# Value products of two quads in one group, eight buffers of transposed probabilities, and later last products in a hybrid attention block

## The chip, the cores and the metric

The kernel runs on one core of a Trainium2 chip. The metric is the device time of one execution in microseconds. Five engines work side by side, each on its own queue of instructions in order: TensorE (PE in the profile; its weight loads are the row PEld), VectorE (DVE), ScalarE (ACT), GpSimd (POOL) and SyncE (SP), which issues nearly all DMA transfers. Semaphores order them among each other.

## The reference, cut to what matters

One encoder layer on 1024 tokens of width 1024: one input projection, two groups of eight attention heads of 64 columns each, a gate, an output projection, a residual and a layer norm.

```python
h = jnp.einsum('bsd,de->bse', x, w_in[layer])
q_a, k_a, v_a, z_a, q_b, k_b, v_b, z_b = jnp.split(h, SPLIT_POINTS, axis=-1)
y_a = neighborhood_attention(q_a, k_a, v_a, rel_pos_bias[layer])      # window 8 x 16 on a 16 x 64 grid
y_b = windowed_gqa_with_sink(rotary(q_b), rotary(k_b), v_b, sink_logits[layer])   # |i - j| <= 128
mixed = jnp.concatenate([y_a * jax.nn.silu(z_a), y_b * jax.nn.silu(z_b)], axis=-1)
y = jnp.einsum('bse,ed->bsd', mixed, w_out[layer])
x = layer_norm(DEEPNORM_ALPHA * x + y, ln_gain[layer], ln_bias[layer])
```

In each attention the probabilities are a softmax over a row's keys, and the output is probabilities times values. Reshapes are left out above.

## The kernel before, in words

Nearly all matmuls are in 16 bits: each operand is split into a high and a low half, and three products (high-high, high-low, low-high) stand for one product in 32 bits. So one block of the input projection is 8 x 3 matmuls of 128x512 (`project`, L381, its matmul L404), and the output projection has the same form (`out_mms`, L1155, its matmul L1165).

**Prologue.** The values of all heads are projected first, the inputs and the weights are scanned for scales (`x_turn`, L514, turns a column of maxima into a row with a matmul against the identity), and six of the 21 blocks of the input projection are made.

**The attention loop** (L1328) runs over 128 units in steps i. A unit is one head and 128 queries: the first 64 units are the windowed group ("b"), the last 64 the neighbourhood group ("a"). Four units that follow each other make a quad. For each unit:

- `stage_mm` (L924, matmul L933) makes the scores of a whole quad in four banks of PSUM, tag "s", of which there are five. A head has 64 columns, so these matmuls use 64 rows of the array, and two heads go side by side on its two halves. `batch(i + 1)` issues them at each step with i % 4 == 3, for the quad that begins at the next step.
- `stage_qk` (VectorE, L958) adds bias or mask and finds the row's extreme, `stage_exp` (ScalarE, L974) takes the exponential, `stage_sum` (VectorE, L980 and L981) the reciprocal of its sum.
- `stage_tr` (L985) splits the probabilities into halves (ScalarE L992, VectorE L993), which frees the bank, and issues a DMA on SP that transposes them into a tile `tr` (L999). A quad has two such tiles; there are BH = 6, those of three quads.
- `stage_pv` (L1005, matmul L1035) multiplies the transposed probabilities of a quad by the values: 18 or 24 matmuls that use 64 columns of the array, two heads side by side. Results lie in one half of the bank "t", by the parity of the quad. `PV_AT` (L1321) says at which step a quad's products are issued: quad q at step 4q + 11, right behind the scores of a later quad; quads 30 and 31 at 131 and 135, where no scores are left.
- `stage_z` (L1037, VectorE L1043 and L1046) multiplies that by the gate, in place, at the steps of `Z_AT`.

**Fill.** Between these groups TensorE works on `fill`, a list of generators: the other 15 blocks of the input projection (48 matmuls each) and then parts of the output projection (`out_head`, L1171). `pump_to(u)` (L1056) issues as many of these matmuls as the table FILL_AT gives for the step u; WARP bends the four steps of a quad. What the loop leaves over goes out at its end (L1414).

**The other engines' queues** are lists as well; `pop` takes a few operations per step, and `need` takes one that is about to be used. Weight blocks are loaded on SP (`w_load`, L200), split on ScalarE (L214) and GpSimd (L219, L220). The output weights come in 16 loads (`wo_load`, L1100) at the steps WO_LD into raw tiles with the tags WO_TAG, and are scanned and split (`wo_split`, L1111). Six of them are loaded earlier too, for their scan only, into four buffers of tag "wos" (`wo_pre_load`, L804); the last two of these scans are at steps 12 and 20. `gather_v` (L846) loads the values of the next head pair for one column block, one step behind the products that were the last to use that block of the pair before.

**The end** (`final`, L1182). Here the order is no longer written out by hand. The gated outputs of the "a" heads are split into m tiles (ScalarE L1076, VectorE L1077), first the tokens below 512, then the rest; the other weights are split (L1121 to L1134, and L1191 on GpSimd); one more bank, tag "t", gets its first half of the sum (12 matmuls); then eight open banks get the second half, one head pair e after the other, three matmuls for each bank and e; then the remaining blocks, the residual (L1215) and the norm.

Of the kernel before, what the change touches and what calls it, by code (L numbers as in the profile page):

```python
# [25 lines left out]
QSCALE = 2.0 ** -15  # L26
BH, BR, NX, F1 = 6, 6, 6, 0.2
NSPLIT, NP = 6, 2
# [12 lines left out]
FILL = ORDER[NPRO:]  # L41
FILL_AT = [0, 6.6, 13.4, 21.4, 29.4, 37.4, 45.4, 53.4, 61.4, 70, 78.8, 87.6, 96.4, 105, 113, 122, 125, 127, 128.5, 131.5, 136]
ZTAG = {"z3": "zv", "zb3": "zc", "z2": "zs", "zb1": "zd", "zb2": "ze"}
# [4 lines left out]
VA_AT = [46, 49, 52, 55]  # L48
WO_TAG = ("wor", "wor", "raw", "raw") + ("wr",) * 5 + ("wor", "wor", "raw", "raw", "raw", "wr", "wr")
M_AT = [64, 72, 80, 88]  # L50
WO_PRE = (9, 10, 12, 13, 14, 15)
WO_POST = (7, 8)
WO_MAX = 88
EO = (4, 5, 6, 7, 0, 1, 2, 3)
LAST = ((0, 384), (384, 128))
# [19 lines left out]
def hybrid_block(ctx, tc, xT, x, wt, wv, wo, bias, sink, gain, lbias, cos, sin, bmask, out):  # L75
# [5 lines left out]
    wp = ctx.enter_context(tc.tile_pool(name="wp", bufs=3))  # L81
# [56 lines left out]
    wos = const.tile([128, 1], F32, name="wos")  # L138
# [297 lines left out]
    with ExitStack() as vctx:  # L436
# [77 lines left out]
        def x_turn(ps):  # L514
            nc.tensor.matmul(ps[:, 320:448], gm.to_broadcast([128, 128]), identf, start=False, stop=True,
                             skip_group_check=True)

# [99 lines left out]
        for k in range(KT):  # L617
# [6 lines left out]
            for ps in FIRST if k == 0 else SECOND if k == 1 else ([(t, a, i) for i in range(3)] for t, a in T1):  # L624
# [5 lines left out]
                if k > 1:  # L630
                    g = T1.index((t, a))
# [200 lines left out]
    rawp = ctx.enter_context(tc.tile_pool(name="rawp", bufs=3, reuse_waits="tile"))  # L832
# [168 lines left out]
    def quad(q):  # L1001
        g, p, j, t = units[4 * q]
        return g, p, t // 2 if g == "b" else t[0]
# [48 lines left out]
    fill.extend(project(n) for n in FILL)  # L1052
    FILL_N = [48] * len(FILL) + [9, 9, 6, 12, 24]
    pumped = [0]

    def pump_to(u):  # L1056
        n = 0
        k = int(u) % 4
        u = int(u) // 4 * 4 + 4 * (WARP[k] + (WARP[k + 1] - WARP[k]) * (u - int(u)))
        for k, c in enumerate(FILL_N):  # L1060
            u0, u1 = FILL_AT[k], FILL_AT[k + 1]
            n += int(c * min(max((u - u0) / (u1 - u0), 0), 1))
        pump(n - pumped[0])
        pumped[0] = max(n, pumped[0])
# [35 lines left out]
    def wo_load(n):  # L1100
        if n < 16:
            tag = WO_TAG[n]
            pool, bufs = (rawp, 3) if tag == "raw" else (wp, {"wr": 5, "wor": 2}[tag])
            raw = pool.tile([128, 512], F32, tag=tag, name=f"wor{n}", bufs=bufs)
            e, a = WO_SEQ[n]
            nc.sync.dma_start(raw, wo[e, :, 512 * a:512 * a + 512])
            wo_raw[n] = raw
# [44 lines left out]

    LO = 10
    NU = len(units)
# [165 lines left out]

    PV_AT = {4 * q + 11: q for q in range(30)}  # L1321
    PV_AT.update({131: 30, 135: 31})
    Z_AT = {4 * q + 13: q for q in range(30) if q not in (24, 25, 28, 29)}
    Z_AT.update({115: 24, 116: 25, 128: 28, 129: 29, 132: 30, 136: 31})

    clock["step"] = 0
    scan_ops = []
    for i in range(-LD, NU + LO):  # L1328
# [15 lines left out]
        if i in PRE_AT:  # L1344
            n = len(WO_PRE) - len(PRE_AT) + PRE_AT.index(i)
# [44 lines left out]
        pump_to(i + F1)  # L1390
        if i - 1 in PV_AT and quad(PV_AT[i - 1])[0] == "a":
            _, p, b = quad(PV_AT[i - 1])
            if p < 3:
                gather_v(p + 1, b)
        free = 2 if i % 4 > 1 or i >= NU else 0
        turned = pop("dve", free if i < 105 else 1 + free)
        if i % 4 == 0 and i < NU:
            stage_exp(units[i])
        if i in PV_AT or i % 4 == 3 and i + 1 < NU:
            if i < NU:  # L1400
                stage_sum(units[i - 1:i + 1])
            pump_to(i + QK_AT)
            if i + 1 < NU:
                batch(i + 1)
            if i in PV_AT:
                stage_pv(PV_AT[i])
            if i + 1 < NU:
                stage_qk(units[i + 1])
# [83 lines left out]
```

## Time and profile before

| | us |
|---|---|
| median of 3 runs | 439.92 |
| lowest and highest of them | 439.67, 441.48 |
| the profiled execution's own time | 441.73 |
| its span, first to last instruction | 439.90 |
| mean granted TensorE clock | 0.998 of full speed |
| first scores of the loop | 122.8 |
| first and last value products | 145.5, 361.7 |

The profile is of one execution. A row of a timeline has the start and the length in us, the engine, the line of the kernel, the operation, the tile written and those read, the shape and the count; what the engine idled for stands in brackets. Rows that follow each other with the same line and shape are merged, and the length is then that of all of them. A length ends at the modelled end of the last instruction; matmuls are pipelined, so the next one starts before that.

### The profile page before, as it was taken

To read this page: it belongs to the slowest core of one execution; us is meant where nothing else is said; L and a number is where in the kernel's file an instruction comes from. 1 tells how busy PE (TensorE), PEld (TensorE's weight loads), DVE (VectorE), ACT (ScalarE), POOL (GpSimd) and SP (SyncE) were. 2 spreads that over 40 slices of the span, in tenths; PEclk is the share of its full clock that TensorE was granted. 3 is DMA by queue.
4 is the path that set the end of the run, shared out by engine and by line. 5 is a ranking of instruction groups with operands and counts; after the bars stand their busy time and mean duration, and the time that the engine had idled before them with its cause. 6 is when DMAs were issued, how large, how long until landed. Compare 5 with 4: busy or idle time off the path is not lost. (4 is left out here: it accounts for less than half of the span.)

```text
span 439.9 us, 8798 instructions
## 1 busy us (share of the span) xinstructions
PE 431.2 (98%) x2955; PEld 233.2 (53%) x2955; DVE 347.8 (79%) x897; ACT 298.8 (68%) x697; POOL 212.7 (48%) x204
## 2 busy tenths in 40 slices
PE   9999999999999999999999999999999989999994
PEld 8987754444444545454545455554545544444442
DVE  5999947929989988988888887887879739089954
ACT  6798359877577988877889899879787756002211
POOL 0305743564845868356333455566652158005840
PEclk9999999999999999999999999999999999999999
DMA  8992088967946978776999899999999979101721
GB/s 296 343 339 71 5 259 250 302 247 254 322 113 136 168 147 171 141 145 143 173 154 201 138 190 223 192 202 217 216 208 225 193 166 363 41 1 72 262 74 72
DMA packets 133981, 81.72 MB, mean 186 GB/s; under 512 B 101296, under 2 KB 113328, under 8 KB 133680
## 3 DMA queue, kind: packets, MB, share of 16 engines
q1 hardware_dynamic: 133504, 80.67, 74.4%
q8 instruction: 23, 0.38, 0.3%
q10 hardware_dynamic: 432, 0.49, 0.3%
q14 instruction: 22, 0.18, 0.1%
HBM read 50.73 MB, written 9.96 MB: 138 GB/s over the span
## 5 line engine op out<-in xcount | busy, mean ns | idle before, releaser
L404 PE MATMUL ps_pj<-xf,wh 128*128 128x512 f16 x672 | 201.2, 379 | 0.0
L404 PE MATMUL ps_pj<-xf,wl 128*128 128x512 f16 x336 | 127.5, 380 | 0.0
L404 PEld LDWEIGHTS <-wh 128*128 128x128 f16 x672 | 64.9, 98 | 75.4 <-issue 0.8
L1165 PEld LDWEIGHTS <-m 128*128 128x128 f16 x408 | 38.7, 98 | 43.7
L974 ACT ACTIVATE ps_s<-sn,nm 128x385 f32<-128x385 f32 (+3 forms) x96 | 52.1, 543 | 13.9 <-DVE nm L958 12.5
L992 ACT ACTIVATE split<-ps_s,ri 128x384 f16<-128x384 f32 (+2 forms) x96 | 48.5, 539 | 18.3 <-ACT ps_s L974 11.7
L993 DVE SCALAR_TENSOR_TENSOR split<-ps_s,ri,split 128x384 f16<-128x384 f32 (+2 forms) x96 | 52.0, 570 | 5.6 <-ACT split L992 4.6
L1165 PE MATMUL ps_s<-wo,m 128*128 128x512 f16 (+1 forms) x240 | 53.3, 374 | 0.0
L404 PEld LDWEIGHTS <-wl 128*128 128x128 f16 x336 | 32.8, 98 | 38.5 <-issue 0.3
L219 POOL TENSOR_SCALAR wr<-wr,wsc 128x512 f32<-128x512 f32 x26 | 22.4, 862 | 46.9 <-ACT wh L214 45.5
L958 DVE CUSTOM_DVE_ANT_0 sn<-ps_s,bm,nsk 128x384 f32<-128x384 f32 (+1 forms) x64 | 39.7, 635 | 6.6 <-PE ps_s L933 6.4
L901 POOL TENSOR_SCALAR bias<-bias,rsg 128x552 f32<-128x552 f32 (+1 forms) x24 | 20.0, 834 | 45.8 <-DMA bias<-in_bias 33.9
L958 DVE CUSTOM_DVE_ANT_0 sn<-ps_s,bias,sg 128x264 f32<-128x264 f32 (+1 forms) x64 | 33.9, 543 | 2.3 <-PE ps_s L933 1.6
L933 PE MATMUL ps_s<-ks,qs 64*128 64x384 f16 (+4 forms) x384 | 33.4, 305 | 0.1
L220 POOL TENSOR_TENSOR wl<-wr,wh 128x512 f16<-128x512 f32 x26 | 31.8, 1223 | 2.2
L1222 ACT ACTIVATE sd<-mv,eps 128x1 f32<-128x1 f32 x8 | 2.4, 295 | 41.8 <-DVE mv L1220 39.5
L1264 POOL TENSOR_TENSOR xr<-xr,gb 128x512 f32<-128x512 f32 x7 | 11.2, 1607 | 35.9 <-ACT xr L1261 35.9
L993 DVE SCALAR_TENSOR_TENSOR split<-px,ri,split 128x384 f16<-128x384 f32 (+2 forms) x32 | 26.0, 812 | 2.5 <-ACT split L992 2.4
L933 PEld LDWEIGHTS <-qs 64*128 64x128 f16 x384 | 16.2, 94 | 19.5 <-issue 13.3
L681 PEld LDWEIGHTS <-xf 128*128 128x128 f16 x216 | 21.0, 98 | 8.5 <-DVE xf L535 0.3
L1165 PE MATMUL ps_pj<-wo,m 128*128 128x512 f16 (+1 forms) x120 | 24.2, 347 | 0.0
L681 PE MATMUL ps_s<-wf,xf 128*128 128x320 f16 x144 | 23.8, 299 | 0.0
(213 smaller groups left out, 791.0 us busy)
## 6 DMA issues: line engine op xcount, KB each, us to landing
ws<-in_wt SPq DMA_DIRECT2D x15, 512.0 KB, 5.2
wr<-in_wt SPq DMA_DIRECT2D x26, 256.0 KB, 2.9
bias<-in_bias SPq DMA_DIRECT2D x16, 276.0 KB, 3.3
wor<-in_wo SPq DMA_DIRECT2D x16, 256.0 KB, 3.6
xr<-in_x SPq DMA_DIRECT2D x8, 512.0 KB, 7.2
xraw<-in_xT SPq DMA_DIRECT2D x15, 256.0 KB, 5.0
out<-xr SPq DMA_DIRECT2D x14, 256.0 KB, 2.0
bias<-in_bias SPq DMA_DIRECT2D x8, 368.0 KB, 3.8
```

What stands on the lines that cost most here:

```text
L219: nc.gpsimd.tensor_scalar(raw, raw, scale, 1.0, op0=ALU.mult, op1=ALU.mult)
L220: nc.gpsimd.tensor_sub(l, raw, h)
L404: nc.tensor.matmul(ps, a[:, k % 4, :], mv, start=(k == 0 and i == 0), stop=(k == KT - 1 and i == 2))
L681: nc.tensor.matmul(ps[:, :320], lh[t // 4, k][:, 128 * (t % 4):128 * (t % 4) + 128], rh[k][:, 320 * a:320 * a + 320], start=(k == first an ...
L901: op = enq("pool", lambda: nc.gpsimd.tensor_scalar(bv, bv, rsg, -1.0, op0=ALU.mult, op1=ALU.mult), ld, prio=0)
L933: nc.tensor.matmul(st[u, "ps"][:, :m], *parts[i], start=i == 0, stop=i == 2)
L958: nc.vector.tensor_tensor_reduce(sn[:, :m], ps[:, :m], bias_t, sg[:, c:c + 1], init, op0=ALU.add, op1=ALU.min, accum_out=nm)
L974: nc.scalar.activation(pt[:, :m], sn[:, :m], AF.Exp, bias=nm, scale=-1.0, accum_out=sm)
L992: nc.scalar.activation(hl[:, :m, 0, :c], src, AF.Copy, scale=ri)
L993: nc.vector.scalar_tensor_tensor(hl[:, :m, 1, :c], src, ri, hl[:, :m, 0, :c], op0=ALU.mult, op1=ALU.subtract)
L1165: nc.tensor.matmul(ps, lh[:, ts], rh[:, cs], start=(e == EO[0] and i == 0), stop=(e == EO[-1] and i == 2))
L1264: nc.gpsimd.tensor_mul(xr[:, h1], xr[:, h1], gb[:, h1])
```

## The change

Value products are issued for two quads at once: quads q and q + 1 (q even) at step 4q + 15, one behind the other; quads 30 and 31 together at step 138. So the even quads come four steps later than before, the odd ones stay, and the last two come seven and three steps later. `Z_AT` follows: 4q + 17 and 4q + 18. BH, the number of tr tiles, goes from 6 to 8. The loop runs four steps longer (LO 10 to 14), and 24 more matmuls of the output projection are given steps (136 to 140.5) in place of being left to the end.

`pump_to` gets a tilt: a triangle over eight steps that runs ahead by up to 0.85 of a step, highest where the products of two quads have just been issued, so the gap before a pair gets more fill and the gap behind it less. A few early entries of FILL_AT move by up to 0.5 of a step.

The raw tiles of output weights use the four "wos" buffers in place of two "wor" buffers and two of the three "raw" ones. `x_turn` is marked as a transpose. The condition of the last step with scores (i + 1 < NU becomes i < NU) lets the sums of the last two units be taken in that step though no single product hangs on it, and `gather_v` runs over both quads of a pair.

```diff
-BH, BR, NX, F1 = 6, 6, 6, 0.2
+BH, BR, NX, F1 = 8, 6, 6, 0.2
...
-FILL_AT = [0, 6.6, 13.4, 21.4, 29.4, 37.4, 45.4, 53.4, 61.4, 70, 78.8, 87.6, 96.4, 105, 113, 122, 125, 127, 128.5, 131.5, 136]
+FILL_AT = [0, 6.6, 13.2, 20.9, 28.9, 37, 45.1, 53.3, 61.4, 70, 78.8, 87.6, 96.4, 105, 113, 122, 125, 127, 128.5, 131.5, 136, 140.5]
...
-WO_TAG = ("wor", "wor", "raw", "raw") + ("wr",) * 5 + ("wor", "wor", "raw", "raw", "raw", "wr", "wr")
+WO_TAG = ("wos",) * 4 + ("wr",) * 5 + ("wos", "wos", "raw", "wos", "wos", "wr", "wr")
...
+TILT = 0.85
...
             nc.tensor.matmul(ps[:, 320:448], gm.to_broadcast([128, 128]), identf, start=False, stop=True,
-                             skip_group_check=True)
+                             is_transpose=True, skip_group_check=True)
...
-    FILL_N = [48] * len(FILL) + [9, 9, 6, 12, 24]
+    FILL_N = [48] * len(FILL) + [9, 9, 6, 12, 24, 24]
...
+        if 12 <= u < 124:
+            u += TILT * (1 - abs((u - 12) % 8 / 4 - 1))
...
-            pool, bufs = (rawp, 3) if tag == "raw" else (wp, {"wr": 5, "wor": 2}[tag])
+            pool, bufs = (rawp, 1) if tag == "raw" else (wp, {"wr": 5, "wos": 4}[tag])
...
-    LO = 10
+    LO = 14
...
-    PV_AT = {4 * q + 11: q for q in range(30)}
-    PV_AT.update({131: 30, 135: 31})
-    Z_AT = {4 * q + 13: q for q in range(30) if q not in (24, 25, 28, 29)}
-    Z_AT.update({115: 24, 116: 25, 128: 28, 129: 29, 132: 30, 136: 31})
+    PV_AT = {4 * q + 15: (q, q + 1) for q in range(0, 30, 2)}
+    PV_AT[138] = 30, 31
+    Z_AT = {4 * q + 17 + k: q + k for q in range(0, 30, 2) for k in range(2)}
+    for n in (24, 25):
+        Z_AT.pop(4 * 24 + 17 + n - 24)
+    Z_AT.update({115: 24, 116: 25, 139: 30, 140: 31})
...
-        if i - 1 in PV_AT and quad(PV_AT[i - 1])[0] == "a":
-            _, p, b = quad(PV_AT[i - 1])
-            if p < 3:
+        for q in PV_AT.get(i - 1, ()):
+            g, p, b = quad(q)
+            if g == "a" and p < 3:
                 gather_v(p + 1, b)
...
-        if i in PV_AT or i % 4 == 3 and i + 1 < NU:
+        if i in PV_AT or i % 4 == 3 and i < NU:
...
-            if i in PV_AT:
-                stage_pv(PV_AT[i])
+            for q in PV_AT.get(i, ()):
+                stage_pv(q)
```

## The prediction

> **What bounds the kernel now.** I read the page's first part, the waits of TensorE, then its timeline.
>
> ```profile
> span 439.9 us, 8798 instructions
> ...
> PE 431.2 (98%) x2955; PEld 233.2 (53%) x2955; DVE 347.8 (79%) x897; ACT 298.8 (68%) x697; POOL 212.7 (48%) x204
> ```
>
> ```profile
> PE ps_t L1247 <- ACT dg L1246: 1.5, 1, 1.5
> PE ps_t L1035 <- DMA tr<-split: 1.5, 1, 1.5
> PE ps_t L443 <- PEq L1481: 0.8, 1, 0.8
> ```
>
> TensorE is busy for 98% of the span, and its waits are three: one at the start, one of 1.5 us for a transposed tile, one at the very end. No other engine reaches 80%. So the kernel gets shorter only where TensorE gets less to do or loses a wait. But "busy" hides something, because the modelled end of a matmul lies some 0.16 us behind the start of the next. Starts tell more. Here is one round of the attention loop: fill matmuls (L404), four units' scores (L933), one quad's value products (L1035), fill again; below it an early round that has scores and no products.
>
> ```profile
> 301.28 0.38 PE L404 MATMUL ps_pj<-xf,wl 128*128 128x512 f16 x1
> ...
> 301.50 0.38 PE L404 MATMUL ps_pj<-xf,wh 128*128 128x512 f16 x1
> ...
> 301.81 1.11 PE L933 MATMUL ps_s<-ks,qs 64*128 64x352 f16 x12
> ...
> 302.27 0.65 PE L933 MATMUL ps_s<-ks,qs 64*128 64x384 f16 x6
> ...
> 302.59 0.33 PE L933 MATMUL ps_s<-ks,qs 64*128 64x384 f16 x2
> ...
> 302.85 0.30 PE L1035 MATMUL ps_t<-tr,va 128*64 128x256 f16 x2
> ...
> 303.58 0.45 PE L1035 MATMUL ps_t<-tr,va 128*64 128x128 f16 x10
> ...
> 303.75 0.28 PE L1035 MATMUL ps_t<-tr,va 128*64 128x128 f16 x4
> ...
> 303.96 0.39 PE L404 MATMUL ps_pj<-xf,wh 128*128 128x512 f16 x1
> ```
>
> ```profile
> 137.79 0.49 PE L933 MATMUL ps_s<-ks,qs 64*128 64x384 f16 x4
> ...
> 138.21 0.39 PE L404 MATMUL ps_pj<-xf,wl 128*128 128x512 f16 x1
> ```
>
> A fill matmul takes 0.22 us from start to start (301.28 to 301.50), yet scores begin 0.31 after the last one: 0.09 more. A pair of 384-column score matmuls takes 0.16 (302.27 to 302.59 is two pairs), so the last ends its stream at 302.75, and the products begin at 302.85: 0.10. A pair of 128-column products takes 0.056 (303.58 to 303.75 is three), so the products stream out at 303.86 and fill begins at 303.96: 0.10. In the early round, two pairs from 137.79 stream out at 138.11 and fill begins at 138.21: 0.10. **Each change between the array's three shapes (128*128, 64*128, 128*64) costs about 0.10 us of TensorE**, from whichever shape to whichever. All rows of the loop that I read have it and otherwise stand back to back.
>
> **The change, part by part.** *Products in pairs.* Before, 32 groups of scores (384 matmuls, 12 each) and 32 groups of products:
>
> ```profile
> L933 PE MATMUL ps_s<-ks,qs 64*128 64x384 f16 (+4 forms) x384 | 33.4, 305 | 0.1
> ```
>
> Shape changes before: 29 rounds with scores and products have 3 each (87), rounds 0, 4 and 8 without products have 2 each (6), the last three product groups stand alone in fill with 2 each (6): 99. After: 14 rounds with scores and a pair (42), 18 rounds of scores alone (36), two pairs alone at steps 127 and 138 (4): 82. That is 17 fewer at 0.10: 1.7 us. The first pair of a product group is also slower (0.30 long against 277 ns, the mean of its form among the groups by shape): 0.02 for 16 groups that now follow another group, 0.3. No row shows products of one quad right behind those of another; it may cost nothing, as between matmuls inside a group, or a full 0.10 (16 times, 1.6). I take nothing, since the shape is the same. The Trainium skill ("TensorEngine Tiling (Array Packing)", "Key Properties") says that changing the tiling mode, not just the tile, drains the engine; by that the cost is nothing too, and by the other end the sum below would shrink to 1.1 us. **Term: -2.0 us.**
>
> *Fill between the rounds.* FILL_AT, WARP and TILT give 13 to 20 fill matmuls after a pair and 25 to 31 in the other gap (17 to 25 in each before). With 0.22 for a fill matmul and about 1.1 for a quad's products, score round follows score round after 6.5 to 7.7 us in both kinds; before 6.6 to 7.5. The number of fill matmuls is unchanged, so they cost nothing in themselves. The waiting room of the softmax is another matter (next term).
>
> *The softmax chain.* Scores need banks that the splits (L993) of the batch before set free. Two rounds:
>
> ```profile
> 294.39 0.94 DVE L993 SCALAR_TENSOR_TENSOR split<-ps_s,ri,split 128x288 f16<-128x288 f32 x2 [0.22 <-ACT split L992]
> 294.57 1.34 PE L933 MATMUL ps_s<-ks,qs 64*128 64x264 f16 x12
> ...
> 295.39 0.21 PEld L933 LDWEIGHTS <-qs 64*128 64x128 f16 x4 [0.33 <-issue]
> ```
>
> ```profile
> 322.91 0.94 DVE L993 SCALAR_TENSOR_TENSOR split<-ps_s,ri,split 128x288 f16<-128x288 f32 x2 [0.22 <-ACT split L992]
> ...
> 323.46 0.96 PE L933 MATMUL ps_s<-ks,qs 64*128 64x264 f16 x12
> ```
>
> ```profile
> 255.00:290.00 35.00, 35.00 (x306) 18.55 (x302) 28.18 (x91) 32.40 (x87) 20.70 (x24) 1.00 1.00 207
> 290.00:325.00 35.00, 34.85 (x282) 17.93 (x282) 28.54 (x92) 27.37 (x72) 21.54 (x24) 1.00 1.07 204
> ```
>
> At 295.33 two splits end and at 295.39 the second half of the scores goes on: TensorE waited about 0.3 us there (12 score matmuls took 1.34, not 0.96). At 323 the splits end at 323.85, when the second half of those scores is due: no slack. The last row group is busy time by stretch (TensorE, weight loads, VectorE, ScalarE, GpSimd): in 255 to 290 us ScalarE works 32.40 of 35 us. So from about 260 on the softmax is nearly as slow as TensorE, and what TensorE saves there, some 5 of the 14 paired rounds at 0.12 and what it arrives early with, is partly handed to this wait. Bounds: nothing lost, or 1.2 us (what the ten pairs up to about 295 have saved, 10 at 0.12). I take **+0.45**, nearer to nothing because ScalarE falls back to 27.37 of 35 us in the next stretch. Two z products (0.48 each) now stand in every second batch in place of one in each; they come behind the splits that free the banks, and have five steps to the next products in place of two.
>
> *The late products.* Now the end of the loop.
>
> ```profile
> 350.36 2.97 PE L1165 MATMUL ps_s<-wo,m 128*128 128x512 f16 x13
> 354.82 1.18 PE L1035 MATMUL ps_t<-tr,va 128*64 128x256 f16 x24 [1.49 <-DMA tr<-split]
> ```
>
> ```profile
> 346.16 12.15 SPq L999 DMA_TRANSPOSE tr<-split x8
> ...
> 355.93 4.92 PE L1165 MATMUL ps_s<-wo,m 128*128 128x512 f16 x22
> ...
> 357.97 1.16 POOL L1134 TENSOR_TENSOR wo<-wor,wo 128x512 f16<-128x512 f32 x1
> ...
> 360.78 1.18 PE L1035 MATMUL ps_t<-tr,va 96*64 96x256 f16 x24
> 361.89 5.57 PE L1165 MATMUL ps_s<-wo,m 128*128 128x512 f16 x25
> 362.01 0.48 DVE L1046 SCALAR_TENSOR_TENSOR z<-ps_t,zcol,z 128x256 f32<-128x256 f32 x1 [5.49 <-PE ps_t L1035]
> ...
> 367.30 2.75 PE L1165 MATMUL ps_t<-wo,m 128*128 128x512 f16 x12
> ...
> 369.89 0.81 PE L1165 MATMUL ps_pj<-wo,m 128*128 128x512 f16 x3
> ```
>
> Quad 30's products at step 131 wait 1.49 us for their transpose while other matmuls are ready behind them in TensorE's order. At step 138 some 55 output matmuls (12 us) stand between the products of quads 28, 29 and those of 30, 31, so the wait goes: **-1.5 us**. The last transposes are issued by 358.31; the products of quad 31 would begin near 361.5, so they find their tile. What is late next: the second of two halves of the output matmuls needs the weights split on GpSimd (L1134 ends 359.13, used near 359.3), just in time. Then the tail. Before, 8.1 us of TensorE work lie between the last products (361.8) and the first matmul that needs the late m tiles (369.89). After, 8 fill matmuls and the 12 on bank t, 4.4 us. VectorE does z of quad 31, then the m and weight splits in its order:
>
> ```profile
> 367.11 0.79 DVE L1131 SCALAR_TENSOR_TENSOR wo<-wor,wos,wo 128x512 f16<-128x512 f32 x1 [0.77 <-ACT wo L1123]
> ...
> 370.96 1.64 DVE L1077 TENSOR_TENSOR m<-z,m 128x512 f16<-128x512 f32 x1
> ```
>
> From 362.01 to 372.60, 10.6 us, 0.8 of it idle, to the second half of the first m tile. The eighth bank of that round (tokens 512 on) reads it 7 banks of 0.65 and two matmuls in: 4.4 + 5.0 = 9.4 us after the products, against about 9.8. **+0.4 us.** Bounds: nothing, or 1.2 with the idle time kept.
>
> *The rest.* x_turn as a transpose:
>
> ```profile
> 28.15 0.49 PE L515 MATMUL ps_s<-identf,gm 128*128 128x128 f32 x2
> 28.40 0.54 PE L627 MATMUL ps_s<-wvh,x 128*128 128x320 f32 x2
> ```
>
> Two passes take 0.25; one is left. Between nothing and 0.25; I take 0.05. Output weights in the scanned tiles' buffers: the same loads at the same steps behind the same splits, and the two scans that must be done first lie at steps 12 and 20, the loads that reuse them at 26 and 30. Nothing. Two gathers of values now go out one behind the other on SP every second round: the same number, and the transposes behind them have slack to their products everywhere but at the end. Nothing.
>
> **Sum:** -2.0 - 1.5 - 0.05 + 0.45 + 0.4 = -2.7 us on the span of 439.9. That execution's own time was 441.73; the median of the runs without profile is 439.92, close to the span, so I subtract from it: **437.2 us**, 0.6% faster. A measurement tells about 0.5% (2.2 us) from no change.
>
> **Rivals.**
> 1. *The softmax chain becomes the bound* from 260 on. For it: splits ending as the scores are due; against: TensorE lost only 0.3 us there. Then 1.2 us of the 2.0 go, and uneven gaps cost 0.2 in four rounds: -2.0 + 1.2 + 0.8 - 1.55 + 0.4 = -1.15, **438.8**. Chance 0.18.
> 2. *The tail takes the wait back.* The weight split of 359.13 is late by 0.6, VectorE keeps its idle 0.8, and both z products start only after quad 31's (0.48): with the 0.4, 2.3 in place of it, -2.0 - 1.55 + 0.45 + 2.3 = -0.8, **439.1**. The Trainium skill ("PSUM — Partial Sum Buffer", "PSUM bank collisions raise a hardware error") says that VectorE must not read a bank while TensorE writes it in the same partitions, even in other columns; by that z of quad 30 must wait for the products of 31, which share bank t, and the tail's term would be 0.9. No row shows a z beside products. Chance 0.12.
> 3. *Slower: the transposes block SP.* The pair frees its tr buffers together, later; if a transpose comes first, SP, in order, holds all that stands behind it, biases too.
>
> ```profile
> 280.68 1.11 PE L933 MATMUL ps_s<-ks,qs 64*128 64x352 f16 x12
> ```
>
> ```profile
> 288.27 1.22 SPq L999 DMA_TRANSPOSE tr<-split x1
> ```
>
> A batch's first transpose goes out 7.6 us after its scores begin; the pair ends 3.2 us after. It decides if that gap falls below 3.2, or if the buffers are not the two quads' further that BH 8 provides. A block of 0.5 us in each of 14 pairs is 7 us, 4.3 more than the 2.7 saved: **444.2**. Chance 0.10.
>
> **How the numbers follow.** The forecast has 0.60, its own range 435.9 to 438.0: the low end is -2.0 - 1.5 - 0.25 with nothing handed back (436.2), less the 0.25 by which the fastest run shown (439.67) lies under the median. The range goes up over rivals 1 and 2 and the product-to-product cost (1.6): 435.9 to 439.8. Faster by over 0.5%: the forecast and a little of rivals 1 and 2, 0.62; within: 0.28; slower: rival 3, 0.10.
>
> **What would show it.** 17 shape changes fewer, products of two quads with no gap between them, no wait on tr at the end: right. Score groups longer than their streams between 260 and 345: rival 1. A hole in TensorE within 15 us behind the last products: rival 2. Transposes sooner than 4 us after the scores, or SP waiting for products: rival 3. The forecast is wrong if the saved changes show up again as equal waits, or if the products of the second quad begin 0.1 late.

## The result, and the profile after

The changed kernel takes **445.4 us** (median of 4 runs, 444.92 to 446.09), the kernel before 440.6 beside it (439.67 to 441.48): ratio 1.0087, 95% interval 1.0059 to 1.0115. The forecast was 437.2, the range 435.9 to 439.8; the change makes the kernel slower. The profiled execution took 446.09 us, its span is 444.30 (before 441.73 and 439.90). The change adds lines, so L404 is now L405, L933 L934, L1035 L1036, L993 L994, L1165 L1168, L872 L873.

First the page's first part and the waits of TensorE (line waited for: us in all, times, longest) of the changed kernel.

```profile
span 444.3 us, 8771 instructions
...
PE 431.7 (97%) x2954; PEld 232.4 (52%) x2954; DVE 345.9 (78%) x897; ACT 298.5 (67%) x697; POOL 210.1 (47%) x204
```

```profile
PE ps_s L262 <- DVE cs L252: 1.7, 1, 1.7
...
PE ps_pj L405 <- POOL wl L221: 1.1, 1, 1.1
PE ps_s L934 <- DVE split L994: 1.0, 4, 0.3
...
PE ps_s L1168 <- POOL wo L1137: 0.5, 1, 0.5
PE ps_pj L1168 <- DVE z L366: 0.4, 1, 0.4
```

The wait for a transposed tile at the end is gone. Others have come, and two of them, for `cs` and `wl`, lie in the prologue, which the change was not expected to touch. The timeline places them: the two prologue waits, the first scores, a pair of products, and the end.

```profile
95.79 0.39 PE L405 MATMUL ps_pj<-xf,wl 128*128 128x512 f16 x1 [1.05 <-POOL wl L221]
...
104.31 0.22 PE L262 MATMUL ps_s<-cs,ones 128*128 128x128 bf16 x1 [1.66 <-DVE cs L252]
...
125.91 0.99 PE L934 MATMUL ps_s<-ks,qs 64*128 64x256 f16 x12
...
314.53 2.17 PE L1036 MATMUL ps_t<-tr,va 128*64 128x256 f16 x48
316.63 0.39 PE L405 MATMUL ps_pj<-xf,wh 128*128 128x512 f16 x1
...
347.56 0.76 PE L934 MATMUL ps_s<-ks,qs 64*128 64x264 f16 x7
348.57 0.53 PE L934 MATMUL ps_s<-ks,qs 64*128 64x288 f16 x5 [0.25 <-DVE split L994]
...
350.49 2.75 PE L1168 MATMUL ps_pj<-wo,m 128*128 128x512 f16 x12 [0.42 <-DVE z L366]
...
366.50 1.46 PE L1168 MATMUL ps_s<-wo,m 128*128 128x512 f16 x6 [0.48 <-POOL wo L1137]
367.88 2.17 PE L1036 MATMUL ps_t<-tr,va 128*64 128x256 f16 x48
369.99 1.90 PE L1168 MATMUL ps_s<-wo,m 128*128 128x512 f16 x8
```

Before, the first scores and the last group of scores (unit 124) began at:

```profile
122.77 0.99 PE L933 MATMUL ps_s<-ks,qs 64*128 64x256 f16 x12
...
343.11 0.88 PE L933 MATMUL ps_s<-ks,qs 64*128 64x264 f16 x12
```

So the span divides into a **prologue** up to the first scores (122.77 before, 125.91 after: +3.14), the **loop** from there to the scores of unit 124 (220.34, 221.65: +1.31), and the **tail** from there to the end of the last matmul (92.31, 92.28: -0.03); what lies behind the last matmul is as long as before (4.50, 4.45). That is the whole +4.4. Inside the loop I sum the time from start to start over all 1723 matmuls by their kind:

| loop, us | before | after |
|---|---|---|
| products (624 matmuls) | 29.84 | 28.12 |
| scores (372) | 30.56 | 33.34 |
| fill (727) | 159.94 | 160.19 |

The products give 1.72 us: the loop has 14 shape changes fewer (the other 3 of the 17 lie in the tail), so 0.12 us each. The scores take 2.78 back, in groups that wait for banks. A group of scores is named below by its first unit, and its time runs from its first start to the start of the next other matmul. Units 44, 48 and 96 had 0.92, 0.92 and 1.27 us and now have 1.51, 1.34 and 1.93; unit 104 has 1.76 in place of 1.04.

### The profile page after: what moved, and what is told of

Its sections match the earlier page's. It is cut to its first block, busy times and chain, and to the rows that moved or that the text cites. A ratio compares the mean times of both kernels' runs of the same rounds, so it can differ in the third digit from the quotient of the medians.

```text
span 444.3 us, 8771 instructions
## 1 busy us (share of the span) xinstructions
PE 431.7 (97%) x2954; PEld 232.4 (52%) x2954; DVE 345.9 (78%) x897; ACT 298.5 (67%) x697; POOL 210.1 (47%) x204
## 5 line engine op out<-in xcount | busy, mean ns | idle before, releaser
L405 PE MATMUL ps_pj<-xf,wh 128*128 128x512 f16 x672 | 201.8, 379 | 0.1
L405 PE MATMUL ps_pj<-xf,wl 128*128 128x512 f16 x336 | 127.5, 379 | 1.1 <-POOL wl L221 1.1
L405 PEld LDWEIGHTS <-wh 128*128 128x128 f16 x672 | 64.5, 98 | 79.1 <-issue 5.3
L1168 PEld LDWEIGHTS <-m 128*128 128x128 f16 x408 | 38.7, 98 | 45.2 <-issue 1.7
L994 DVE SCALAR_TENSOR_TENSOR split<-ps_s,ri,split 128x384 f16<-128x384 f32 (+2 forms) x96 | 52.0, 570 | 9.8 <-ACT split L993 9.0
L993 ACT ACTIVATE split<-ps_s,ri 128x384 f16<-128x384 f32 (+2 forms) x96 | 48.5, 540 | 10.7 <-ACT ps_s L975 4.7
L405 PEld LDWEIGHTS <-wl 128*128 128x128 f16 x336 | 32.8, 98 | 40.6 <-issue 1.8
L1168 PE MATMUL ps_s<-wo,m 128*128 128x512 f16 (+1 forms) x240 | 53.3, 374 | 0.5 <-POOL wo L1137 0.5
L902 POOL TENSOR_SCALAR bias<-bias,rsg 128x552 f32<-128x552 f32 (+1 forms) x24 | 19.0, 790 | 48.3 <-DMA bias<-in_bias 36.3
L934 PE MATMUL ps_s<-ks,qs 64*128 64x384 f16 (+4 forms) x384 | 35.7, 305 | 1.3 <-DVE split L994 1.0
L934 PEld LDWEIGHTS <-qs 64*128 64x128 f16 x384 | 16.5, 94 | 22.6 <-issue 16.6
L994 DVE SCALAR_TENSOR_TENSOR split<-px,ri,split 128x384 f16<-128x384 f32 (+2 forms) x32 | 25.4, 794 | 2.8 <-ACT split L993 2.7
L981 DVE TENSOR_SCALAR ps_s<-sm 128x2 f32<-128x2 f32 x64 | 10.3, 161 | 20.9 <-ACT ps_s L975 20.6
L1168 PE MATMUL ps_pj<-wo,m 128*128 128x512 f16 (+1 forms) x120 | 24.4, 347 | 0.4 <-DVE z L366 0.4
```

What stands on the lines that cost most here:

```text
L405: nc.tensor.matmul(ps, a[:, k % 4, :], mv, start=(k == 0 and i == 0), stop=(k == KT - 1 and i == 2))
L902: op = enq("pool", lambda: nc.gpsimd.tensor_scalar(bv, bv, rsg, -1.0, op0=ALU.mult, op1=ALU.mult), ld, prio=0)
L934: nc.tensor.matmul(st[u, "ps"][:, :m], *parts[i], start=i == 0, stop=i == 2)
L993: nc.scalar.activation(hl[:, :m, 0, :c], src, AF.Copy, scale=ri)
L994: nc.vector.scalar_tensor_tensor(hl[:, :m, 1, :c], src, ri, hl[:, :m, 0, :c], op0=ALU.mult, op1=ALU.subtract)
L1168: nc.tensor.matmul(ps, lh[:, ts], rh[:, cs], start=(e == EO[0] and i == 0), stop=(e == EO[-1] and i == 2))
```

## The experiments

Ratios are to the kernel before, run on the same chip beside each; its medians there were 440.87 to 441.61. Prologue, loop and tail are those of the profiled execution, cut as above; behind the tail lie another 4.1 to 4.6 us of the span. The profiled execution is one of the kernel's runs, and not always a typical one: for e2_notilt, e3_oldfill and b_fill it was the shortest of ten, for e10_zb3 the longest of ten, for e12_pairs the eleventh of twelve. So a difference between two kernels' stages is to be held against their ratios.

| kernel | median | ratio (95%) | prologue | loop | tail | span |
|---|---|---|---|---|---|---|
| before | 440.6 | 1 | 122.77 | 220.34 | 92.31 | 439.9 |
| after | 445.4 | 1.0087 (1.0059-1.0115) | 125.91 | 221.65 | 92.28 | 444.3 |
| e1_layout | 442.06 | 1.0019 (1.0001-1.0038) | 122.41 | 221.56 | 91.74 | 439.9 |
| b_buf | 444.69 | 1.0064 (1.0040-1.0088) | 125.77 | 220.56 | 92.41 | 443.3 |
| b_late | 439.58 | 0.9952 (0.9926-0.9978) | 122.38 | 220.36 | 90.53 | 437.8 |
| e2_notilt | 440.94 | 0.9986 (0.9963-1.0010) | 122.18 | 221.53 | 90.73 | 438.6 |
| e3_oldfill | 439.39 | 0.9961 (0.9938-0.9984) | 122.42 | 218.53 | 90.85 | 436.4 |
| e5_noscan | 440.82 (one run) | - | 122.66 | 221.70 | 90.54 | 439.0 |
| e6_half | 439.19 | 0.9963 (0.9945-0.9981) | 122.47 | 219.04 | 90.96 | 437.0 |
| e7_zspread | 442.87 (one run) | - | 122.15 | 221.36 | 93.41 | 441.1 |
| b_fill | 443.80 | 1.0050 (1.0030-1.0070) | 122.55 | 222.38 | 92.02 | 441.1 |
| e8_tilt | 441.59 | 1.0001 (0.9981-1.0021) | 122.35 | 220.60 | 92.13 | 439.2 |
| e10_zb3 | 440.07 | 0.9952 (0.9931-0.9972) | 123.17 | 221.21 | 91.00 | 439.5 |
| e11_port | 440.89 | 0.9979 (0.9957-1.0001) | 122.64 | 221.19 | 91.02 | 439.0 |
| e12_pairs | 439.62 | 0.9959 (0.9942-0.9975) | 122.41 | 220.57 | 91.17 | 438.7 |
| e13_single | 439.83 | 0.9962 (0.9944-0.9980) | 122.52 | 219.73 | 90.52 | 437.3 |

### The prologue: the buffers

e1_layout is the changed kernel with three raw buffers again, so that everything behind them in memory lies where it lay before.

```diff
-            pool, bufs = (rawp, 1) if tag == "raw" else (wp, {"wr": 5, "wos": 4}[tag])
+            pool, bufs = (rawp, 3) if tag == "raw" else (wp, {"wr": 5, "wos": 4}[tag])
```

> The changed kernel with three raw buffers in place of one, so that the six split tiles lie where they lay before. Theory (placement): GpSimd's clearing of the split tiles no longer waits 3.7 us for the stores of the values (vd<-vt), TensorE loses nothing at 95.8 and 104.3 us, and the first scores begin near 122.8 in place of 125.9: about 3.0 us less than the changed kernel, 442.4, still some 1.5 us over the kernel before. Rival (the marked transpose of x_turn or the order of the loads makes the start late): the first scores stay at 125.9 and the time at 445.4.

b_buf is the other side: the kernel before with the new tags and buffer counts and nothing else.

```diff
-WO_TAG = ("wor", "wor", "raw", "raw") + ("wr",) * 5 + ("wor", "wor", "raw", "raw", "raw", "wr", "wr")
+WO_TAG = ("wos",) * 4 + ("wr",) * 5 + ("wos", "wos", "raw", "wos", "wos", "wr", "wr")
...
-            pool, bufs = (rawp, 3) if tag == "raw" else (wp, {"wr": 5, "wor": 2}[tag])
+            pool, bufs = (rawp, 1) if tag == "raw" else (wp, {"wr": 5, "wos": 4}[tag])
```

> The kernel before with the output weights in the wos buffers and one raw buffer, and nothing else of the change. Theory (placement): the clearing of the split tiles waits for the stores of the values, and the first scores begin 3.0 us later, near 125.9; all else is as before: 443.5. Rival (something else in the change makes the start late): 440.5, as before.

The one edit removes the loss (122.41), the other alone makes it (125.77). How it comes about can be read on GpSimd's timeline: after, before, and e1_layout.

```profile
84.66 1.34 POOL L221 TENSOR_TENSOR wl<-wr,wh 128x512 f16<-128x512 f32 x1
89.68 4.14 POOL L873 MEMSET split<- 128x768 f16 x6 [3.69 <-DMA vd<-vt]
...
94.58 1.15 POOL L221 TENSOR_TENSOR wl<-wr,wh 128x512 f16<-128x512 f32 x1
```

```profile
84.52 1.34 POOL L220 TENSOR_TENSOR wl<-wr,wh 128x512 f16<-128x512 f32 x1
85.80 4.13 POOL L872 MEMSET split<- 128x768 f16 x6
```

```profile
84.15 1.34 POOL L221 TENSOR_TENSOR wl<-wr,wh 128x512 f16<-128x512 f32 x1
85.43 4.13 POOL L873 MEMSET split<- 128x768 f16 x6
```

The six `split` tiles are cleared once, by GpSimd. After the change this waits 3.69 us for a DMA that stores `vt`, a tile of values from the prologue. The memset has nothing to do with that DMA's data; the wait is one for memory that both use at different times. That `split` has moved onto `vt` because the raw pool is two buffers (4 KB a partition) smaller, I infer from the pair of runs; no view shows addresses. Behind the memset stand the weight splits: `wl` comes at 95.73 (94.58 + 1.15), and TensorE takes it at 95.79. A weight tile's load and scan follow late in turn, as ScalarE's timeline has it:

```profile
101.46 1.06 ACT L773 ACTIVATE junk<-ws 128x1024 bf16<-128x1024 f32 x1 [2.70 <-DMA ws<-in_wt]
```

and the scale made from it is the second wait, at 104.31. The two are 1.22 and 1.82 us by TensorE's starts (start to start, less a fill matmul): 3.04 of the 3.14.

### The tail: the late products

b_late is the kernel before with the last products alone moved, in single quads everywhere else.

```diff
-    LO = 10
+    LO = 14
...
-    PV_AT.update({131: 30, 135: 31})
+    PV_AT = {i: (q,) for i, q in PV_AT.items()}
+    PV_AT[138] = 30, 31
...
-    Z_AT.update({115: 24, 116: 25, 128: 28, 129: 29, 132: 30, 136: 31})
+    Z_AT.update({115: 24, 116: 25, 128: 28, 129: 29, 139: 30, 140: 31})
```

> The kernel before with the products of quads 30 and 31 together at step 138, the z products at 139 and 140, the loop four steps longer and 24 more output matmuls given steps; no other pairs, no other buffers. Theory (the wait comes back): the 1.5 us wait for the transposed tile goes, and two changes of shape (0.2), but the weight split on GpSimd of which the changed kernel shows a wait of 0.6 us is late here too: 1.0 us less than before, 439.5. Rival (the 0.6 was due to the softmax of the changed kernel, which ran late): 1.7 less, 438.8.

The tail falls from 92.31 to 90.53, 1.78 us, and the ratio puts the gain at 2.1 us, nearer to the rival's 1.7 than to the theory's 1.0. The waits of TensorE show nothing but those of the kernel's two ends:

```profile
PE ps_t L1247 <- ACT dg L1246: 1.5, 1, 1.5
PE ps_t L443 <- PEq L1482: 0.8, 1, 0.8
```

So the move does what it should, and gives nothing back. What the changed kernel lost there (0.59 before 350.49, 0.64 before 366.50, 0.66 in the last score group) came from other parts of the change.

### The loop: fill table and tilt

e2_notilt is e1_layout with TILT 0, so that the rounds are as uneven as the pairs make them (score round follows score round after 5.7 to 9.2 us by turns).

```diff
-TILT = 0.85
+TILT = 0
```

> The changed kernel with three raw buffers (as in e1_layout) and TILT 0: the gaps before and behind a pair get the same number of fill matmuls. Theory (uneven rounds): the gap with a pair is 2 us longer than the other, the scores after the short gap wait for the softmax in nearly every second round, 0.5 to 1 us each: 6 us more than e1_layout, 448. Rival (the tilt itself costs: fill that runs ahead brings the tanh of zb3 to ScalarE before the last rotary product has read the cosines, and ScalarE waits 2.7 us at 202): the waits at 207 and 214 us (0.8) go and nothing else comes: 441.6.

The uneven rounds cost nothing, where the theory had 6 us: the loop is as long as with the tilt (221.53, 221.56) and the tail 1.0 us shorter. The rival has the time about right and the reason wrong: without the tilt, too, ScalarE waits 2.7 us at the tanh, and units 44 and 48 still take 1.50 and 2.20. e3_oldfill takes back the moved entries of the fill table as well.

```diff
-FILL_AT = [0, 6.6, 13.2, 20.9, 28.9, 37, 45.1, 53.3, 61.4,
+FILL_AT = [0, 6.6, 13.4, 21.4, 29.4, 37.4, 45.4, 53.4, 61.4,
```

> e2_notilt with the early entries of FILL_AT as they were before (13.4, 21.4, 29.4 and so on). Theory (fill that runs ahead meets the cosines): the tanh of zb3 comes 0.4 of a step later, ScalarE waits for the rotary product on GpSimd 2.0 us or less in place of 2.7, and the score groups of units 44 and 48, 1.50 and 2.20 us long, shrink to about 1.2 each; 1.0 to 1.3 us less than e2_notilt. Rival (the pairs themselves make these groups wait): they stay at 1.5 and 2.2, and the time is that of e2_notilt.

The loop falls by 3.0, to 218.53, which is 1.8 less than in the kernel before. Both executions are the shortest of their ten; the ratios, 0.9986 and 0.9961, put the step at 1.1 us. The mechanism is in the timelines at the group of unit 44; first after, then before (rows of GpSimd, ScalarE and TensorE).

```profile
203.80 1.27 POOL L337 TENSOR_TENSOR rp_raw<-rp_raw,cos 128x512 f32<-128x512 f32 x1
...
205.10 0.69 ACT L365 ACTIVATE z<-ps_pj,invt 128x512 f32<-128x512 f32 x1 [2.73 <-POOL rp_raw L337]
205.69 1.04 ACT L993 ACTIVATE split<-ps_s,ri 128x384 f16<-128x384 f32 x2
206.30 1.14 DVE L994 SCALAR_TENSOR_TENSOR split<-ps_s,ri,split 128x384 f16<-128x384 f32 x2 [2.87 <-ACT split L993]
...
206.39 0.84 PE L934 MATMUL ps_s<-ks,qs 64*128 64x384 f16 x7
...
207.49 0.48 PE L934 MATMUL ps_s<-ks,qs 64*128 64x256 f16 x5 [0.26 <-DVE split L994]
```

```profile
199.78 1.05 ACT L992 ACTIVATE split<-ps_s,ri 128x384 f16<-128x384 f32 x2 [0.48 <-ACT ps_s L974]
...
200.60 1.26 POOL L336 TENSOR_TENSOR rp_raw<-rp_raw,cos 128x512 f32<-128x512 f32 x1
...
201.90 0.69 ACT L364 ACTIVATE z<-ps_pj,invt 128x512 f32<-128x512 f32 x1 [0.48 <-POOL rp_raw L336]
...
203.31 0.99 PE L933 MATMUL ps_s<-ks,qs 64*128 64x384 f16 x12
```

The tanh of the gate block zb3 (L365; a block of the input projection, so part of the fill) writes into the buffer that held the cosines, and GpSimd is the last to read these. Up to 0.4 of a step earlier in the fill table, the block is done earlier and its tanh comes earlier in ScalarE's order, ahead of GpSimd's last read: ScalarE stands 2.73 us in place of 0.48. The tanh itself starts no earlier (79.1 us behind the first scores before, 79.2 after). What has changed is that two splits of the softmax, which came before it (199.78), now come behind it (205.69); VectorE's splits follow them, and TensorE waits for the banks.

b_fill asks whether the table alone does it, in the kernel before with single products, and e10_zb3 whether it is this block: e2_notilt with only the two entries that frame zb3 put back.

```diff
-FILL_AT = [0, 6.6, 13.4, 21.4, 29.4, 37.4, 45.4, 53.4, 61.4,
+FILL_AT = [0, 6.6, 13.2, 20.9, 28.9, 37, 45.1, 53.3, 61.4,
```

> The kernel before with only the early entries of the fill table moved (13.4 to 13.2, 21.4 to 20.9, and so on up to 53.4 to 53.3). Theory A (the moved entries alone send the tanh of zb3 to ScalarE while GpSimd's rotary product still holds the cosines' buffer, whatever the products do): ScalarE waits about 2.7 us at the tanh (L364), the score groups of units 44 and 48 lengthen from 0.92 to 1.3 or more, and from first scores to the scores of unit 124 the loop takes 221.5 to 223.5 us (220.34 before): span 441 to 443. Rival B (it takes the pairs too: with single products the softmax of that time has slack): groups 44 and 48 stay at 0.92, the loop at 220.3, span 439.9.

```diff
-FILL_AT = [0, 6.6, 13.2, 20.9, 28.9, 37, 45.1, 53.3, 61.4,
+FILL_AT = [0, 6.6, 13.2, 20.9, 28.9, 37.4, 45.4, 53.3, 61.4,
```

> The changed kernel with three raw buffers, TILT 0 and all moved fill entries but the two that frame the block zb3 (37.4 and 45.4 as before, in place of 37 and 45.1). With all entries moved the loop took 221.53, with none moved 218.53. Theory A (the tanh of zb3 that waits for the cosines' buffer starts the loss): its wait falls from 2.7 to about 0.5 us, score groups 44 and 48 go back to 0.92, the loop takes 218.6 to 219.8 and the span is 436.5 to 437.7. Rival B (the other moved entries carry it): wait and groups stay as with all moved (1.50, 2.20), span 438.6.

b_fill: the wait is 2.6 us, units 44 and 48 take 1.50 and 1.26, unit 96 2.06, the loop 222.38, the median 0.5% up. The table alone does it. e10_zb3: the wait falls to 0.5 and unit 44 back to 0.92, by the theory; but the loop stays at 221.21 in the profiled execution, a miss. Unit 48 has 1.53, and units 88 and 96 take 1.60 and 2.41. That execution was the longest of its ten, though, and the ratio, 0.9952, is no worse than e3_oldfill's 0.9961: over all runs the two entries bring back as much as the whole table. So the block zb3 explains unit 44; whether it explains the rest of the table's cost stays open, since the runs and the one profile point different ways.

e8_tilt puts the tilt back on e3_oldfill (its TILT line reversed).

> The changed kernel with three raw buffers as before and the old early fill entries, but with TILT 0.85 (the kernel with TILT 0 had a span of 436.4, loop 218.53, 90.85 from there to the last matmul). Theory A (the tilt costs about 1 us, at the end of the loop alone): loop 218.5 to 219, score group of unit 124 near 1.5 in place of 0.81, a wait of about 0.6 for z3 (L366), tail 91.7: span 437.3 to 437.8. Rival B (the tilt's cost came from the late softmax of the new fill entries): group 124 at 0.81, span 436.4. Rival C (the tilt shortens the loop, as it was made for): loop below 218.2, span below 436.

It costs more than the theory had, 1.8 us by the ratios: the tilt runs the fill ahead just as the table did, ScalarE's wait at the tanh is 2.7 us again, unit 44 takes 1.93, the last score group 1.74 in place of 0.81, and TensorE waits 0.59 for the gate block z3 behind it. Loop +2.07, tail +1.28 against e3_oldfill. Why the last group is late under the tilt was not followed further.

### The loop: what is late at unit 96

Three kernels tried reasons for the waits that remain. e5_noscan leaves the eight scans of output weights out of ScalarE; e7_zspread moves the gate product z of each pair's second quad four steps later; e6_half makes pairs in the first half of the loop only.

```diff
-                scan_ops.append(enq("act", lambda n=n: wo_scan(n), load_ops["wo", n]))
+                nc.gpsimd.memset(wom[:, n:n + 1], 0.0)
```

> e2_notilt without eight of the scans of the output weights on ScalarE (about 0.8 us each, between 225 and 285 us); their maxima are put to zero, so this part of the computation is left out. Theory (the softmax chain is the bound from unit 76 on, through ScalarE): the score group of unit 96, 2.26 us long, shrinks to 1.3 or less and those of 76 to 92 to their bare 0.81 to 1.04; the loop from the first scores to those of unit 124 takes 220.3 in place of 221.5. Rival (the chain is held by VectorE or by transfers there, not by ScalarE): group 96 stays over 2.0 us.

```diff
-    Z_AT = {4 * q + 17 + k: q + k for q in range(0, 30, 2) for k in range(2)}
+    Z_AT = {4 * q + 17 + 4 * k: q + k for q in range(0, 30, 2) for k in range(2)}
```

> e2_notilt with the z product of the odd quad of each pair four steps later (4q + 21), so that each batch has one z on VectorE again in place of two and none. Theory (the two z products in one batch delay the softmax): the score group of unit 96 shrinks from 2.26 to about 1.8. Rival (ScalarE's load alone sets it): it stays over 2.1.

```diff
-    PV_AT = {4 * q + 15: (q, q + 1) for q in range(0, 30, 2)}
+    PV_AT = {4 * q + 15: (q, q + 1) for q in range(0, 16, 2)}
+    PV_AT.update({4 * q + 11: (q,) for q in range(16, 30)})
```

> e3_oldfill with pairs for quads 0 to 15 alone (the windowed group), single products at 4q + 11 for quads 16 to 29, and quads 30 and 31 together at step 138. Theory (a pair pays where the softmax has slack): eight pairs save 8 times 0.12, 1.0 us, in full, the late products 1.8: 2.8 us less than the kernel before, ratio 0.9937, if the waits at units 44 and 48 go; 0.9955 if half of them stays. Rival (pairs cost as much as they save anywhere): no faster than b_late, ratio 0.9952 or above.

Less load on ScalarE (30.43 us of work between 255 and 290 in place of 32.44) changes nothing in the one execution (unit 96: 2.46, loop 221.70); that theory falls. Spread z products help unit 96 only to 1.79 and bring a wait of 2.9 us at the end, where a product now meets a bank that is not read yet:

```profile
PE ps_t L1036 <- DVE z L1047: 2.9, 1, 2.9
```

e6_half, on the old fill table, has unit 96 at 0.81, half of the saving (28.85 us of products) and nearly the median of e3_oldfill; its ratio of 0.9963 is what the rival had, pairs that pay nowhere.

What differs at unit 96 is one instruction of VectorE in the chain that frees its banks. The first fence is e2_notilt, the second e3_oldfill, from rows of GpSimd and VectorE.

```profile
290.01 1.16 POOL L1153 TENSOR_TENSOR m<-z,m 128x512 f16<-128x512 f32 x1
290.41 1.18 DVE L994 SCALAR_TENSOR_TENSOR split<-px,ri,split 128x384 f16<-128x384 f32 x1
```

```profile
288.22 0.61 DVE L994 SCALAR_TENSOR_TENSOR split<-px,ri,split 128x384 f16<-128x384 f32 x1
288.32 1.52 POOL L1153 TENSOR_TENSOR m<-z,m 128x512 f16<-128x512 f32 x1
```

Whichever of the two starts second takes longer: the split 1.18 for 0.61, or GpSimd's subtraction 1.52 for 1.16. e11_port moves that subtraction away and leaves the rest of e2_notilt as it is.

```diff
+            late = lambda h=h, o=o: m_ops[e].append(enq("pool", lambda h=h: nc.gpsimd.tensor_sub(
...
+        if i == 98:
+            for late in m_late:
+                late()
```

> The changed kernel with three raw buffers, TILT 0, all fill entries moved, and one more edit: the two GpSimd subtractions of the last of the four early m tiles (L1153) are queued at step 98 in place of right behind their casts at step 88. With them there, VectorE's split of a tile in SBUF (L994, 128x384) took 1.18 us at 290.4 while GpSimd's subtraction ran from 290.0 to 291.2; with the old fill entries the order was the other way round, the split took 0.61 and GpSimd's 1.52. Theory A (the two engines can't read two operands at the same time, and this one collision makes the group of unit 96 late): the split takes 0.61, group 96 shrinks from 2.26 to 1.2 to 1.7 us, span 437.6 to 438.1. Rival B (the softmax is simply late from groups 44 and 48 on): group 96 stays at 2.2 whatever that split takes, span 438.6.

```profile
290.85 0.61 DVE L994 SCALAR_TENSOR_TENSOR split<-px,ri,split 128x384 f16<-128x384 f32 x1
...
294.23 0.51 PE L934 MATMUL ps_s<-ks,qs 64*128 64x264 f16 x6
...
294.95 0.95 PE L934 MATMUL ps_s<-ks,qs 64*128 64x288 f16 x6 [0.21 <-DVE split L994]
```

The split takes 0.61 and unit 96 falls from 2.26 to 1.61, by the theory; the loop gains 0.34 of the 0.65, since unit 120 takes 0.25 more in that execution and units 64 and 80 another 0.07. The span of 439.0 misses the theory's 437.6 to 438.1, and the median, 440.89, is e2_notilt's. In e10_zb3, too, the splits in question are long: 1.50 us at 276.56, ahead of unit 88, and 1.17 at 290.83, ahead of unit 96.

### Do the pairs pay?

Two of the shortest kernels, e3_oldfill with pairs and b_late with single products, were put side by side once more as e12_pairs and e13_single.

> Once more the changed kernel with three raw buffers, the old early fill entries and TILT 0, beside the next kernel on one chip. Theory A (17 fewer shape changes are worth 1.7 us in the loop once nothing else is disturbed): median 1.2 to 2.0 us below that of the next kernel. Rival B (what the pairs save goes back through later waits): medians within 0.6 us of each other.

> Once more the kernel before with the late last products alone, products of single quads, 97 shape changes. Both theories: about 2.1 us below the kernel before (ratio 0.995); they differ in its distance from the kernel with pairs (1.2 to 2.0 us above it by theory A, within 0.6 by rival B).

The medians are 439.62 and 439.83, within 0.6 of each other, as the rival had it. e12_pairs is the same program as e3_oldfill, and its profiled span is 2.3 us longer. This time GpSimd came first at unit 96, and a bias tile landed late before unit 120:

```profile
288.20 1.15 POOL L221 TENSOR_TENSOR wl<-ws,wh 128x512 f16<-128x512 f32 x1
...
288.57 1.20 DVE L994 SCALAR_TENSOR_TENSOR split<-px,ri,split 128x384 f16<-128x384 f32 x1
...
331.56 0.88 POOL L902 TENSOR_SCALAR bias<-bias,rsg 128x736 f32<-128x736 f32 x1 [2.44 <-DMA bias<-in_bias]
...
332.47 0.62 DVE L959 CUSTOM_DVE_ANT_0 sn<-ps_s,bias,sg 128x384 f32<-128x384 f32 x1 [1.62 <-POOL bias L902]
```

Unit 96 takes 2.19 there against 1.22 in e3_oldfill, unit 120 2.12 against 1.04. So unit 96 is partly a matter of the execution, and the 1.0 us of it in the step from e2_notilt to e3_oldfill was not the fill table's own. Units 44 and 48 do belong to the table. With the whole moved table (after, e1_layout, e2_notilt, e5_noscan, e11_port, b_fill) unit 44 takes 1.50 to 1.52 and unit 48 1.26 to 2.20; in e7_zspread, where z comes later, they take 1.12 and 2.21. On the old table without the tilt they take 0.92 and 0.92 to 1.01.

The score groups of the loop sum to 30.49 and 32.51 us in the two executions with pairs, 30.59 and 29.96 in those with single products: on the mean 1.2 more, against 1.72 less in the products. The tail is 90.85 and 91.17 with pairs, 90.53 and 90.52 without, 0.5 more, most of it waits for the gate block z3 (0.27 and 0.58 by TensorE's starts). So 0.0 of the 1.72 is left. Two executions of each are few, and the two with pairs lie far apart: one keeps nearly all of the saving in its loop, the other none. But the mean agrees with the medians: on the whole, what the pairs save, the softmax and what hangs on it take back. Why z3 is later with pairs stays open.

## Why the prediction was wrong, step by step

In spans the forecast was -2.7 and the outcome +4.4. The 7.1 us between them are 3.2 in the prologue (forecast -0.05), 2.9 in the loop (forecast -2.0 + 0.45) and 1.1 in the tail (forecast -1.5 + 0.4), each rounded.

- **"Output weights in the scanned tiles' buffers ... Nothing": the step that failed most.** It asked when the buffers come free and not what moves in memory when a pool shrinks. Price: 3.1 us, in a stage that the diff does not name. Shown by e1_layout and b_buf; that the cleared tiles lie on `vt` is inferred.
- **"The number of fill matmuls is unchanged, so they cost nothing in themselves": failed.** True of the matmuls (159.94 and 160.19 us in the loop), and the prediction left the rest to its softmax term, which counts banks and no tanh. But a block's place in the fill table is also when ScalarE gets its tanh, and the moved entries and the tilt both put it ahead of GpSimd's last read of the cosines. Price in the loop: about 2 us for the table (b_fill) or for the tilt (e8_tilt), in the changed kernel 2.78 of score groups in all, of which unit 96's part depends on the execution.
- **Shape changes, -2.0: right.** 99 became 82, 17 fewer. The 14 of them in the loop gave 29.84 - 28.12 = 1.72 us, 0.12 each: the 0.10 of a change and the 0.02 of a slower first pair. A second quad's products behind the first cost no change: 48 take 2.10 us (314.53 to 316.63) where twice 24 took 2.22 (360.78 to 361.89). The Trainium skill ("TensorEngine Tiling (Array Packing)", "Key Properties") says that it is the mode's change that drains the engine; the traces agree.
- **The softmax chain, +0.45: the right wait, too small, and for a reason that did not hold.** The prediction put it down to ScalarE's load, which in the one execution of e5_noscan made no difference. With all else mended the score groups take back 0.2 of the 1.72 in one execution and 2.2 in the other; that the mean, 1.2, is the bound of rival 1 is chance. In the second of these executions the banks came late by a collision of VectorE with GpSimd and by a late bias tile, neither of which the prediction looked at. That the saved changes show up again as waits is what the prediction itself gave as a sign of being wrong.
- **Late products, -1.5: right,** 1.78 measured (b_late): the wait, 1.56 by TensorE's starts, and two shape changes, which the prediction has in its -2.0.
- **Tail, +0.4: too dear.** b_late has no wait there. The wait for the output weights that rival 2 priced at 0.6 did come in the changed kernel, at 0.64; in the mended kernels with pairs 0.19 and 0.14 of it are left, so most of it came with the late softmax. Rival 2's rule from the Trainium skill ("PSUM — Partial Sum Buffer", "PSUM bank collisions raise a hardware error") fits the changed kernel: z of both quads starts at 370.10, behind the last product, as VectorE's row below says, and not behind its own quad's. Whether bank or program sets that, no run separates.

```profile
370.10 0.88 DVE L1047 SCALAR_TENSOR_TENSOR z<-ps_t,zcol,z 128x256 f32<-128x256 f32 x2 [8.49 <-PE ps_t L1036]
```

- **x_turn, -0.05: not visible in the time.** One pass fewer is there (28.30 to 28.38 in place of 28.15 to 28.40), but the first scores of the mended kernels with it begin at 122.15 to 123.17, of those without at 122.38 to 122.77.
- **Rival 3 did not come.** In the changed kernel no product waits for its tile, and SyncE's transposes wait 10.4 us in all behind value products, 10.2 before. That its 444.2 lies near the measured 445.4 is chance.

## What to carry to other kernels

A buffer count is also a memory layout: when a pool shrinks, look in the waits of every stage for a write that waits for a DMA whose data it does not use, and put the size back to see whether the time follows. A table that sets when a matmul block is issued also sets when the engines behind it get their operands, so ask what else holds the block's output buffer at the new moment, and what stands behind the waiting instruction in its queue. And where the engine next in line has no slack, a microsecond saved on the bound engine should be counted as saved only after a run beside the version without it: here 1.72 us of TensorE were 0.2 us between two medians, less than the runs can tell from nothing. And a profile is one execution: look where its time lies among the runs before reading a difference of 1 to 2 us between two profiles.

## What the runs showed of the hardware

VectorE's split of a tile in SBUF (two operands in SBUF) and GpSimd's subtraction of two SBUF operands do not run beside each other at full speed: 0.61 us alone and 1.18 or 1.20 beside it; 1.16 alone and 1.52 for GpSimd when the split came first. The rows of a tile in PSUM differ: in the kernel before, the same split of a tile in PSUM (128x384) took 0.60 to 0.62 us all 60 times, 17 of them begun while a two-operand instruction of GpSimd (TENSOR_TENSOR) ran, and the split of the tile in SBUF took 1.16 on the mean of the ten begun so. The Trainium skill ("SBUF — State Buffer", "Who interferes with whom") says that a VectorE instruction with two SBUF inputs and a GpSimd instruction that reads SBUF exclude each other, and that the order of issue decides which one waits; these rows agree. What was not expected is its size in the end: the same program ran with a span of 436.4 us in one execution and of 438.7 in another, and 1.0 of the 2.3 us between them is the score group behind that one split. Of such a group's delay, e11_port took away 0.65 us with the collision.
